# Scores of the first heads set in a fixed order between the last gate products, and the gate and branch instructions around them recorded in program order

## The chip, the cores and the metric

One core of a Trainium2 chip runs the whole program. The metric is the time of one execution in microseconds (us); smaller is better. The engines are PE (matrix multiply), ACT (scalar engine), DVE (vector engine), POOL (GpSimd) and SP, which here only issues DMAs; each works through its own list of instructions in order.

## The reference

One layer of a hybrid encoder, sequence 1024, width 1024, float32:

```python
h = rms_norm(x, norm1)
proj = h @ w_in                       # q, k, v of 16 heads, forget logits, 2 x 1024 gate columns
o_a = forgetting_attention(...)       # 8 causal heads of 64, with cumulated log-forget terms ("fox")
o_b = chunk_band_attention(...)       # 8 heads of 64, own chunk and 8 chunks before, relative bias
g_a, g_b = split(sigmoid(gates), 2)
merged = g_a * (o_a @ w_branch_a) + g_b * (o_b @ w_branch_b)
x = x + merged @ w_out
x = x + square(relu(rms_norm(x, norm2) @ w_up)) @ w_down
return rms_norm(x, final_norm)
```

## The kernel before

**Precision.** Every float32 operand is held as two float32r halves, high and low: `split` writes the high half with an ACT cast and the low half with a subtraction on DVE or POOL. `split_w` does the same to a weight block of 128x512: `wh_...` is cast on ACT, `wl_...` is subtracted on POOL. A product is then three matmuls for each block of 128 rows (high x high, high x low, low x high); 4 blocks make the 12 matmuls that the text counts.

**Stages in order.** Projections to q, k, v; eight gate units; attention of 16 heads (8 of the chunk kind, then 8 of the fox kind); the branch products; the output products (`o`); the feed-forward part. The projections and gates are Strassen products of 7 products of 12 matmuls each for a 2x2 block (operands B11, T1 to T4, B21, B22; weights A11, S1 to S4, A12, A22), accumulated in four PSUM banks `u{unit}_{n}`. A generator, `strassen_steps`, yields after each of the seven. The finished quarter of a gate goes through `gate_out` (`zt`): times `rstd`, a sigmoid on ACT, a store to `z_dram`.

**The gate tail.** Units 6 and 7 are taken last. Unit 7 does its first two products (A11 x B11, S2 x T2), then unit 6 runs `EARLY` = 6 steps. Then T2 and B11 are freed, and in their place `qk` tiles of the first two heads are loaded on POOL's queue. `shifts` computes for a head the scores (`s`, 12 matmuls), reduces each to a minimum on DVE (`mn`), transposes it on PE (`mt`), splits it (`mr`) and stores it to `m_rows`. Attention subtracts it from its own scores (`st`, on PE, with operands `qk` and `sk`) before the exponential (`p`, on ACT), and multiplies by the values (`pv`).

**The branch products.** `branch(pool, b, c, h)` makes `m{c}_{h}_{b}`: weights `wr` are loaded by SP, split to `wh_ab{c}_{b}` and `wl_ab{c}_{b}`, multiplied with the attention output `oh`, `ol` (24 matmuls for both h), and the result is multiplied by the gate `z` on DVE. The branch b = 0 goes between the fox heads as `fillers`; b = 1 comes after attention: there POOL adds (`m`), ACT casts (`mh`), POOL subtracts (`ml`), and `mh`, `ml` are the operands of the output products. Attention's last pair of heads is normalised by `on` (DVE, with `rb` loaded from `r_dram`), stored to `o_dram` by ACT's queue, loaded as `olt` and split to `oh`, `ol`.

**What sets the order.** A scheduler places the instructions of each engine when the program is built; dependences and the order of writing guide it. An engine wrapped by `Ordered` (VO, TO, AO, LO) keeps its instructions among each other in the order in which the program writes them:

```python
return lambda *a, **kw: tc.keep_in_program_order(getattr(self.eng, name)(*a, **kw))
```

Each such instruction has the line of this helper in the profile (L96 before, L95 after). Tiles live in rings: `wr` has 4 buffers (RAW), `wh` and `wl` 6 each (HL).

Of the kernel before, what the change touches and what calls it, by code (L numbers as in the profile page):

```python
# [18 lines left out]
P = 128  # L19
# [12 lines left out]
EARLY_GATES = 2  # L32
START1 = (0,)
START2 = (0, 1, 2, 3)
EARLY, AHEAD = 6, 2
LO_POOL = lambda n: False

BC, PB = 2, 5
# [2 lines left out]

NORM = (2, 6, 10, 14)
BIAS = 1
GPOOL = (7,)

LEAD, XB, XR = 3, 4, 6

# [30 lines left out]
def hs(h):  # L78
    return slice(h * HALF, (h + 1) * HALF)
# [3 lines left out]
def hybrid_block(ctx: ExitStack, tc: tile.TileContext, xT, g1, wall, wf, fb, relb, relt, rows, g2, g3, outT):  # L83
# [20 lines left out]
    def psum(stack, name, bufs):  # L104
        return stack.enter_context(tc.tile_pool(name=name, bufs=bufs, space=PSUM, reuse_waits="tile"))
# [106 lines left out]
    def product(bank, first, pairs, part=False, eng=T):  # L212

        n = len(pairs) * 3
        t = 0
        for w, x in pairs:
            for wi, xi in ((0, 0), (0, 1), (1, 0)):
                eng.matmul(bank, w[wi], x[xi], start=(first and t == 0), stop=(t == n - 1 and not part),  # L218
                         skip_group_check=part or not first)
                t += 1  # L220
# [91 lines left out]
    for h in range(2):  # L312
# [36 lines left out]
    def gate_out(ps, c, h, eng=V):  # L349
        t = etile("zt")  # L350
        eng.tensor_tensor(t, ps, rstd[:, hs(h)], op=ALU.mult)
        A.activation(t, t, AF.Sigmoid)
        store(z_dram[c, :, hs(h)], t)

    def norm1():
# [79 lines left out]
        load_r(qk, qk_dram[2 * pr + hh])  # L435
        return qk

    def shifts(pr, hh, qk, bc, ps_s, ps_t):

        fox = pr >= 4  # L440
        mn = aps.tile([P, 8], F32, tag="mn", name=f"mn{pr}_{hh}", bufs=2)
        for i in range(8):
            j0 = 0 if fox else max(0, i - 4)
            W = (i + 1 - j0) * P
            st = aps.tile([P, 4], F32, tag="st", name="st", bufs=4)
            prev, x = 3.0e38, 0
            for s0, n, v in pieces(W):
                ks = j0 * P + s0
                ps = ps_s.tile([P, HALF], F32, tag="d", name="s")
                diag = fox and s0 + v == W  # L450
                T.matmul(ps[:, :n], qk[:, 1, i * P:(i + 1) * P], qk[:, 0, ks:ks + n], start=True, stop=not diag)  # L451
# [6 lines left out]
                V.tensor_tensor_reduce(ps[:, :v], ps[:, :v], bc[:, b0:b0 + v], 1.0, prev, ALU.add, ALU.min, out)  # L458
# [4 lines left out]
        T.transpose(pt[0:8, 0:P], mn, ident)  # L463
# [7 lines left out]
        for _ in strassen_steps(*args, **kw):  # L471
            pass

    def strassen_steps(u, ps_pool, mk, out, start=(), between=None, before=None, cut=0):
# [9 lines left out]
        for b in (0, 2, 3, 1) if between else range(4):  # L484
            banks[b] = ps_pool.tile([P, HALF], F32, tag="d", name=f"u{u}_{b}")
        p1, u2, c22 = mk("p1"), mk("u2"), mk("c22")
        steps = [(n, range(4)) for n in range(7)]
        if start:
            more = (0, 4, 1, 2, 3, 5, 6) if between else range(7)
            steps = [(n, range(3)) for n in start] + [(n, (3,) if n in start else range(4)) for n in more]  # L490
        for i, (n, ks) in enumerate(steps):
            if i >= cut:
                yield
            if cut and i == cut:
                ws = strassen_w(u, G, ALL[cut:])
            wn, xn, b, first = PRODS[n]
            wh, wl = ws[wn]
            product(banks[b], first and 0 in ks, [((wh[:, k, :], wl[:, k, :]), xop[xn, k]) for k in ks],
                    3 not in ks)
            if 3 not in ks:  # L500
                continue
            if n == 3 and before:
                before[0]()
            if n == 0:
                A.copy(p1, banks[0])
            elif n == 1:
                V.tensor_tensor(u2, banks[1], p1, op=ALU.add)
            elif n == 2:
                V.tensor_tensor(c22, banks[2], u2, op=ALU.add)
            elif n == 3:  # L510
                V.tensor_tensor(c22, banks[3], c22, op=ALU.add)
                out(1, 1, c22)
            elif n == 4:
                if between:
                    between()
                out(0, 0, banks[0])
            else:
                t = mk("cc")
                V.tensor_tensor(t, banks[b], u2, op=ALU.add)  # L519
                out(*((0, 1) if n == 5 else (1, 0)), t)  # L520
        if before:
            before[1]()
            for a in late:
                out_(*a)
# [37 lines left out]

        return finish

    def project_gate(g, **kw):
        return strassen_steps(U_GATE + g, psd[1 - next(units) % 2], etile,
                              lambda row, h, src: gate_out(src, 2 * g + row, h,
                                                          G if g in GPOOL and (row, h) != (0, 0) else V), **kw)

    project_qk(0)  # L570
    for i in range(4):
# [22 lines left out]
    apq = [pool(astack, f"apq{n}", "right") for n in range(2)]  # L594
    for n in range(2):
# [15 lines left out]
    ap_, apv, apq2, ap0 = [pool(astack, n, "right") for n in ("ap", "apv", "apq2", "ap0")]  # L611
    apq.append(apq2)
    psg = psum(astack, "psg", 1)
    pss = psum(astack, "pss", 3)
# [5 lines left out]
    def branch(ps_pool, b, c, h):  # L620

        if h == 0:
            ab_w[b, c] = [split_w(quarter(U_AB + c // 2, ((0, 1), (3, 2))[c % 2][b]), f"ab{c}_{b}")]
        (wh, wl), = ab_w[b, c]
        g = (1 - b) * 8 + c
        z = tmp("z")
        load(z, z_dram[g, :, hs(h)])
        ps = dense(ps_pool, f"m{c}_{h}_{b}", [(wh[:, k, :], wl[:, k, :]) for k in range(4)],
                   [(oh[:, k, hs(h)], ol[:, k, hs(h)]) for k in range(4)])
        V.tensor_tensor(z, ps, z, op=ALU.mult)  # L630
        return z
# [4 lines left out]
        c, h = fillers.pop(0)  # L636
        store(m_dram[c, :, hs(h)], branch(psg, 0, c, h))


    v3 = [apv.tile([P, 8, 3, HD], F32R, tag=f"v3{hh}", name=f"v3{hh}") for hh in range(2)]  # L640
    for hh in range(2):
        V.memset(v3[hh][:, :, 2, :].bitcast(F32), 1.0)

    sks = [ap_.tile([SK, 2, S], F32R, tag=f"sk{n}", name=f"sk{n}") for n in range(2)]

    def load_rest(pr, hh):
        sk = sks[hh]
        if pr % 4 == 0:
            load_r(sk[HD:SK - 2], rows[pr // 4, 0:16])
            load_r(sk[SK - 2:SK, 0, :], rows[pr // 4, 16:18, 0, :])  # L650
        load_r(sk[0:HD], sk_dram[2 * pr + hh])
        load_r(v3[hh][:, :, 0:2, :].rearrange("p c a d -> p c (a d)"), v_dram[pr, hh])
        load_r(sk[SK - 2:SK, 1, :], m_rows[2 * pr + hh])
        return sk

    lo_n, acc_o = [0], {}

    def attend(pr, hh, sk, qk, nb):
# [4 lines left out]
        for h in range(2):  # L663
# [5 lines left out]
            for n, (j, b0, b1) in enumerate(chunks):  # L669
# [28 lines left out]
                A.activation(p[:, c], ps[:, c], AF.Exp, scale=-1.0, bias=ncq[:, j, head:head + 1] if fox else 0.0)  # L698
# [37 lines left out]
                split((oh[:, pr, hs(h)], ol[:, pr, hs(h)]), o, G)  # L736

    forget_columns()
    rest, steps = load_rest(*heads[0]), iter(())
    for n, hd in enumerate(heads):  # L740
        sk, more = rest, iter(())
        if n < 15:
            rest = load_rest(*heads[n + 1])
        if n < 14:
            tiles.append((load_head(*heads[n + 2]), *load_bias(*heads[n + 2])))
            more = shifts(*heads[n + 2], *tiles[-1][:2], pss, psg)
# [370 lines left out]
```

## Time and profile before

| | |
|---|---|
| median of 3 runs | 1561.5 us (1555.68 to 1564.74) |
| the profiled execution | 1553.71 us, its span 1551.9 us (1.8 us lie around it) |
| granted clock of PE, mean | 0.976 |
| busy in the span | PE 1469.4 us (95%), DVE 1018.2 (66%), POOL 919.3 (59%), ACT 735.3 (47%) |

Times within the span are counted from its start. A matmul's row gives the time from issue to its modelled end (0.39 us with 512 columns), while the next is issued earlier: its start minus the start of the row before is what a matmul costs in a row. A row of an engine shows in brackets the idle time before it and what ended it. A row that ends in "xN" stands for N instructions.

### The profile page before, as it was taken

The numbers are of one execution on the slowest core, as the hardware profiler recorded it, in microseconds if no ns is written. First come the engines' busy times: TensorE is split into PE (matmuls) and PEld (weight loads), VectorE is DVE, ScalarE is ACT, GpSimd is POOL, SyncE is SP. The second block draws the span as 40 slices with busy tenths as digits, with TensorE's granted clock in tenths as the row PEclk, the third lists the DMA queues.
The fourth block names the chain that finished last, engine by engine and source line by source line (L and its number), as shares of the span: only waits on it lengthen the run. The fifth ranks groups of instructions, "written<-read, shape, count | busy, mean of one in ns | idle before, by whom it ended". The sixth has DMA issues, their size and how long they took to land.

```text
span 1551.9 us, 21027 instructions
## 1 busy us (share of the span) xinstructions
PE 1469.4 (95%) x6788; PEld 1212.7 (78%) x6788; DVE 1018.2 (66%) x1543; ACT 735.3 (47%) x1379; POOL 919.3 (59%) x735
## 2 busy tenths in 40 slices
PE   6798999999979998999999999999999899999996
PEld 4586888888858787888787888888888688888885
DVE  8989555753356787875422687666666546999644
ACT  5543333334327786766623554333333344444653
POOL 6886776869871222211048378888877445467553
PEclk9799999999989999999999999999999999999998
DMA  4155667774395777885466624444443757489353
GB/s 151 55 150 124 187 186 198 213 214 141 119 270 146 150 166 159 214 214 151 140 196 197 203 68 156 154 152 149 156 151 136 268 187 227 140 251 225 101 188 124
DMA packets 150320, 262.92 MB, mean 169 GB/s; under 512 B 21880, under 2 KB 39544, under 8 KB 147072
## 3 DMA queue, kind: packets, MB, share of 16 engines
q1 hardware_dynamic: 75968, 136.79, 29.0%
q10 hardware_dynamic: 50304, 84.24, 17.0%
q0 software_dynamic: 23936, 40.54, 11.8%
q8 instruction: 53, 0.87, 0.2%
q14 instruction: 59, 0.48, 0.1%
HBM read 175.19 MB, written 86.31 MB: 169 GB/s over the span
## 4 chain that ended last, share of the span: by engine, by line
PE 40%; POOL 3%; DMA 3%; DVE 2%; issue 2%; ACT 1%; SPq 0%; ACTq 0%; DVEq 0%; POOLq 0%
PE u L218 19%; PE dS L218 11%; PE dA L218 5%; PE o L218 4%; POOL wl_A L167 1%; POOL m L785 1%; POOL ml L269 1%; DMA xT<-a_dram 1%; DMA z<-z_dram 1%; PE dA L96 0%; DMA wr<-wall 0%; DMA rb<-r_dram 0%; DVE B22l L269 0%; DVE T2l L269 0%; DMA r_dram<-d 0%
## 5 line engine op out<-in xcount | busy, mean ns | idle before, releaser
L167 POOL TENSOR_TENSOR wl_A<-wr,wh_A 128x512 fp32r<-128x512 f32 x121 | 172.4, 1432 | 61.7 <-ACT wh_A L165 44.2
L167 POOL TENSOR_TENSOR wl_S<-S,wh_S 128x512 fp32r<-128x512 f32 x105 | 146.6, 1399 | 38.3 <-ACT wh_S L165 38.0
L269 DVE TENSOR_TENSOR tl<-p,th 128x512 fp32r<-128x512 f32 (+1 forms) x192 | 110.6, 597 | 29.4 <-ACT th L268 24.5
L165 ACT CAST wh_A<-wr 128x512 fp32r<-128x512 f32 x105 | 65.1, 620 | 103.0 <-DMA a_dram<-at 52.5
L165 ACT CAST wh_S<-S 128x512 fp32r<-128x512 f32 x105 | 64.0, 619 | 78.4 <-PE u L218 33.1
L167 POOL TENSOR_TENSOR wl_S<-ks,wh_S 128x512 fp32r<-128x512 f32 x48 | 68.7, 1512 | 53.8 <-ACT wh_S L96 53.8
L268 ACT CAST th<-p 128x512 fp32r<-128x512 f32 (+1 forms) x192 | 92.3, 508 | 12.2 <-PE pv L702 6.3
L458 DVE CUSTOM_DVE_ANT_0 s<-s,bc 128x384 f32<-128x384 f32 (+3 forms) x128 | 69.6, 562 | 35.2 <-PE s L451 18.5
L451 PE MATMUL s<-qk 128*128 128x384 f32 (+2 forms) x192 | 64.5, 368 | 23.7 <-DMA qk<-qk_dram 13.7
L519 DVE TENSOR_TENSOR cc<-u,u 128x512 f32<-128x512 f32 x70 | 47.9, 686 | 54.9 <-PE u L218 54.6
L188 POOL TENSOR_TENSOR S<-wr,wr 128x512 f32<-128x512 f32 x36 | 51.7, 1436 | 45.4 <-DMA wr<-wall 38.1
L167 POOL TENSOR_TENSOR wl_A<-ka,wh_A 128x512 fp32r<-128x512 f32 x32 | 45.2, 1422 | 47.1 <-ACT wh_A L96 47.1
L880 ACT ACTIVATE v<-v 128x512 f32<-128x512 f32 x64 | 40.5, 632 | 67.4 <-DVE v L879 64.6
L686 PE MATMUL st<-sk 82*128 82x512 f32 (+1 forms) x192 | 66.5, 347 | 1.1 <-DMA sk<-m_rows 1.1
L678 PE MATMUL st<-qk 128*128 128x512 f32 (+1 forms) x192 | 66.9, 352 | 0.2 <-ACT p L698 0.2
L701 PE MATMUL pv<-th,v 128*128 128x512 f32 (+1 forms) x192 | 65.6, 342 | 1.1 <-ACT on L714 0.6
L703 PE MATMUL pv<-tl,v 128*128 128x512 f32 (+1 forms) x192 | 65.4, 340 | 0.9 <-DVE tl L269 0.8
L702 PE MATMUL pv<-th,v 128*64 128x512 f32 (+1 forms) x192 | 65.0, 339 | 0.0
L268 ACT CAST qkh<-qk 128x512 fp32r<-128x512 f32 x32 | 19.9, 621 | 95.1 <-DMA qk_dram<-qkl 41.2
L698 ACT ACTIVATE p<-st,ncq 128x512 f32<-128x512 f32 (+1 forms) x96 | 54.1, 598 | 21.2 <-PE st L694 15.4
L451 PEld LDWEIGHTS s<-qk 128*128 128x128 f32 x192 | 36.8, 201 | 33.1 <-issue 7.9
L208 POOL TENSOR_TENSOR S<-wr,S 128x512 f32<-128x512 f32 x35 | 49.6, 1418 | 17.8 <-DMA wr<-wall 14.3
(378 smaller groups left out, 5082.5 us busy)
## 6 DMA issues: line engine op xcount, KB each, us to landing
wr<-wall SPq DMA_DIRECT2D x243, 256.0 KB
qk<-qk_dram POOLq DMA_DIRECT2D x16, 1024.0 KB, 6.1
a_dram<-at ACTq DMA_DIRECT2D x64, 256.0 KB
xT<-a_dram SPq DMA_DIRECT2D x64, 256.0 KB
qk_dram<-qkh ACTq DMA_DIRECT2D x96, 128.0 KB
a_dram<-v ACTq DMA_DIRECT2D x48, 256.0 KB
xB<-a_dram SPq DMA_DIRECT2D x44, 256.0 KB
z_dram<-zt ACTq DMA_DIRECT2D x32, 256.0 KB
```

Of the source, the lines that this page charges most:

```text
L165: act.copy(wh, src)
L167: G.tensor_tensor(wl, src, wh.bitcast(F32), op=ALU.subtract)
L218: eng.matmul(bank, w[wi], x[xi], start=(first and t == 0), stop=(t == n - 1 and not part), skip_group_check=part or not first)
L268: A.copy(dst[0], src)
L269: eng.tensor_tensor(dst[1], src, dst[0].bitcast(F32), op=ALU.subtract)
L451: T.matmul(ps[:, :n], qk[:, 1, i * P:(i + 1) * P], qk[:, 0, ks:ks + n], start=True, stop=not diag)
L458: V.tensor_tensor_reduce(ps[:, :v], ps[:, :v], bc[:, b0:b0 + v], 1.0, prev, ALU.add, ALU.min, out)
L678: T.matmul(ps[:, c], qk[:, 0, keys], qk[:, 1, qs], start=True, stop=False)
L686: T.matmul(ps[:, c], sk[:, 0, keys], sk[:, 1, qs], start=False, stop=not extra)
L701: T.matmul(pv[:, c], v3[hh][:, j, 1:3, :], th[:, c], start=first, stop=False)
L702: T.matmul(pv[0:HD, c], v3[hh][:, j, 0, :], th[:, c], start=False, stop=False)
L703: T.matmul(pv[:, c], v3[hh][:, j, 1:3, :], tl[:, c], start=False, stop=last)
```

## The change

1. `EARLY` goes from 6 to 3; unit 7, unit 6 and the `shifts` of the first two heads issue their matmuls through `TO`, so that PE keeps the order written. Two scores and then four stand between products.
2. PSUM is shared out anew for the gate tail: one bank `psl`, four `psu`, three `psa` for scores. `strassen_steps` takes its banks one by one.
3. The first head's `sk` and `v3` tiles move to the pool `ap1`, in the place of T2 and B11, and are loaded on POOL's queue before the last gate weights; the load of its row of minima is a call of its own (`load_shift`).
4. GPOOL is dropped: all `zt` products go to DVE.
5. The sigmoids of unit 7 and the first exponentials are issued through `AO`. So is the cast in `split_w` for all branch weights.

```diff
-EARLY, AHEAD = 6, 2
+EARLY, AHEAD = 3, 2
...
-GPOOL = (7,)
...
-    last = project_gate(7, cut=2)
+    pstack.close()
+    lstack = ExitStack()
+    psl, psu, psa = [psum(lstack, n, b) for n, b in (("psl", 1), ("psu", 4), ("psa", 3))]
+    last = project_gate(7, [psl, psa, psu, psu], cut=2, eng=TO)
     next(last)
-    steps = project_gate(6)
+    steps = project_gate(6, [psu] * 4, eng=TO)
     for _ in range(EARLY):
         next(steps)
     xtop.close()
     apq = [pool(astack, f"apq{n}", "right") for n in range(2)]
+    ap1 = pool(astack, "ap1", "right")
...
+    head_tiles(ap1)
     for n in range(2):
         tiles[n] = (load_head(*heads[n]), *tiles[n])
-    ahead = chain(*[shifts(*heads[n], *tiles[n][:2], psd[1], psd[1]) for n in range(2)])
+    rest = load_rest(*heads[0])
+    ahead = chain(*[shifts(*heads[n], *tiles[n][:2], psa, psa, TO) for n in range(2)])
     for _ in chain(steps, last):
         for _ in range(AHEAD):
             next(ahead, None)
     for _ in ahead:
         pass
-    pstack.close()
+    load_shift(*heads[0])
+    lstack.close()
...
-            ab_w[b, c] = [split_w(quarter(U_AB + c // 2, ((0, 1), (3, 2))[c % 2][b]), f"ab{c}_{b}")]
+            ab_w[b, c] = [split_w(quarter(U_AB + c // 2, ((0, 1), (3, 2))[c % 2][b]), f"ab{c}_{b}", AO)]
...
-                A.activation(p[:, c], ps[:, c], AF.Exp, scale=-1.0, bias=ncq[:, j, head:head + 1] if fox else 0.0)
+
+                exp = (A if pr or hh or h or n else AO).activation
+                exp(p[:, c], ps[:, c], AF.Exp, scale=-1.0, bias=ncq[:, j, head:head + 1] if fox else 0.0)
```

**PE in the gate tail.** Before, around the first score of the first head (`s` on `qk0_0`), which stands behind the sixth product (B22 with S4) of unit 6:

```order
L218 MATMUL u6_2_3856<-B22h_130,wl_6_S4_3848 128x512
L451 MATMUL s_3967<-qk0_0_3943 128x256
L218 MATMUL u6_3_3857<-T4h_122,wh_6_A22_3850 128x512
L218 MATMUL u6_3_3857<-T4l_126,wh_6_A22_3850 128x512
L218 MATMUL u6_3_3857<-T4h_122,wl_6_A22_3852 128x512
```

And at the end of the tail, where all scores of the second head (`qk0_1`) follow the last gate product:

```order
L218 MATMUL u7_3_3782<-T4h_122,wl_7_A22_4024 128x512
L463 MATMUL mt_4108<-ident_66,mn0_0_3965 8x128
L451 MATMUL s_4134<-qk0_1_3945 128x256
L451 MATMUL s_4138<-qk0_1_3945 128x256
L451 MATMUL s_4160<-qk0_1_3945 128x384
L451 MATMUL s_4164<-qk0_1_3945 128x512
```

Now the first score stands behind the third product (T1 with S1) of unit 6, three products earlier:

```order
L95 MATMUL u6_2_3918<-T1h_154,wl_6_S1_3843 128x512
L95 MATMUL s_3934<-qk0_0_3910 128x256
L95 MATMUL s_3938<-qk0_0_3910 128x256
L95 MATMUL u6_3_3941<-T3h_146,wh_6_S3_3846 128x512
L95 MATMUL u6_3_3941<-T3l_150,wh_6_S3_3846 128x512
```

and the last of the second head ahead of unit 7's last product:

```order
L95 MATMUL s_4195<-qk0_1_3912 128x256
L95 MATMUL mt_4198<-ident_66,mn0_1_4101 8x128
L95 MATMUL u7_3_4110<-T4h_122,wh_7_A22_4083 128x512
L95 MATMUL u7_3_4110<-T4l_126,wh_7_A22_4083 128x512
```

So scores that stood in a block behind the gates stand between the gate products, while the load of `qk` keeps its place on POOL (behind `wl_6_S4`).

**ACT after attention.** `wh_ab{c}_1` are the casts of b = 1 weights, `mh` the casts of the sums. Before, the last two of the eight weight casts stand ahead of the first `mh`, and then only `mh` follow:

```order
L268 CAST oh_4217<-olt_8352 128x512
L165 CAST wh_ab6_1_8648<-wr23_1_8646 128x512
L165 CAST wh_ab7_1_8696<-wr23_2_8694 128x512
L268 CAST mh0_8322<-m_8356 128x512
```

Now `wh_ab7_0`, the last of b = 0, stands behind the store of the normalised heads, `wh_ab0_1` behind all casts of `olt`, and each later one behind both `mh` of the c before:

```order
L755 DMA o_dram_102<-on7_1_8049 128x512
L95 CAST wh_ab7_0_8271<-wr23_3_8269 128x512
...
L267 CAST oh_4240<-olt_8364 128x512
L95 CAST wh_ab0_1_8372<-wr20_1_8370 128x512
L671 DMA m_dram_106<-z_8292 128x512
L267 CAST mh0_8334<-m_8368 128x512
L267 CAST mh1_8329<-m_8395 128x512
L95 CAST wh_ab1_1_8420<-wr20_2_8418 128x512
L267 CAST mh0_8334<-m_8416 128x512
L267 CAST mh1_8329<-m_8443 128x512
L95 CAST wh_ab2_1_8468<-wr21_1_8466 128x512
```

What moved: seven weight casts, from ahead of the sums to one between each two pairs of sums.

**POOL and PE after attention.** On POOL the same order, before:

```order
L167 TENSOR_TENSOR wl_ab4_1_8554<-wr22_1_8550,wh_ab4_1_8552 128x512
L167 TENSOR_TENSOR wl_ab5_1_8602<-wr22_2_8598,wh_ab5_1_8600 128x512
L785 TENSOR_TENSOR m_8356<-m_8356,z_8364 128x512
L167 TENSOR_TENSOR wl_ab6_1_8650<-wr23_1_8646,wh_ab6_1_8648 128x512
```

and now:

```order
L166 TENSOR_TENSOR wl_ab0_1_8374<-wr20_1_8370,wh_ab0_1_8372 128x512
L807 TENSOR_TENSOR m_8368<-m_8368,z_8376 128x512
L268 TENSOR_TENSOR ml0_8335<-m_8368,mh0_8334 128x512
L807 TENSOR_TENSOR m_8395<-m_8395,z_8397 128x512
L268 TENSOR_TENSOR ml1_8330<-m_8395,mh1_8329 128x512
L166 TENSOR_TENSOR wl_ab1_1_8422<-wr20_2_8418,wh_ab1_1_8420 128x512
```

PE before takes the products of four c at once (here the second half, h = 1):

```order
L218 MATMUL m0_1_1_8387<-oh_4217,wh_ab0_1_8360 128x512
L218 MATMUL m1_1_1_8435<-oh_4217,wh_ab1_1_8408 128x512
L218 MATMUL m2_1_1_8483<-oh_4217,wh_ab2_1_8456 128x512
L218 MATMUL m3_1_1_8531<-oh_4217,wh_ab3_1_8504 128x512
```

and now one c after the other; two matmuls of each h need only `wh`, the other ten of each stand behind the first that needs `wl`:

```order
L217 MATMUL m1_0_1_8426<-oh_4240,wh_ab1_1_8420 128x512
L217 MATMUL m1_0_1_8426<-ol_4241,wh_ab1_1_8420 128x512
L217 MATMUL m1_1_1_8447<-oh_4240,wh_ab1_1_8420 128x512
L217 MATMUL m1_1_1_8447<-ol_4241,wh_ab1_1_8420 128x512
L217 MATMUL m1_0_1_8426<-oh_4240,wl_ab1_1_8422 128x512
```

What moved: four c in parallel became one c at a time, each behind its own `wl`.

More of the change, by code (lines that the diff above doesn't have):

```diff
@@ L348, in hybrid_block, with gate_out @@
         store(c_dram[:, hs(h)], z)
[L349 removed]
+    def gate_out(ps, c, h, act=A):
         t = etile("zt")
[L351 to L352 removed]
+        V.tensor_tensor(t, ps, rstd[:, hs(h)], op=ALU.mult)
+        act.activation(t, t, AF.Sigmoid)
         store(z_dram[c, :, hs(h)], t)
@@ L436, in load_head, with shifts @@
         return qk
-    def shifts(pr, hh, qk, bc, ps_s, ps_t):
+    def shifts(pr, hh, qk, bc, ps_s, ps_t, T=T):
         fox = pr >= 4
@@ L472, in strassen_unit, with strassen_steps @@
             pass
-    def strassen_steps(u, ps_pool, mk, out, start=(), between=None, before=None, cut=0):
+    def strassen_steps(u, ps_pool, mk, out, start=(), between=None, before=None, cut=0, eng=T):
         ws = strassen_w(u, G, ALL[:cut] if cut else FIRST if between else ALL)
@@ L483, in strassen_steps, with bank @@
         banks = {}
-        for b in (0, 2, 3, 1) if between else range(4):
-            banks[b] = ps_pool.tile([P, HALF], F32, tag="d", name=f"u{u}_{b}")
+        def bank(b):
+            if b not in banks:
+                banks[b] = (ps_pool[b] if isinstance(ps_pool, list) else ps_pool).tile(
+                    [P, HALF], F32, tag="d", name=f"u{u}_{b}")
+            return banks[b]
+        for b in (0, 2, 3, 1) if between else () if isinstance(ps_pool, list) else range(4):
+            bank(b)
         p1, u2, c22 = mk("p1"), mk("u2"), mk("c22")
@@ L497, in strassen_steps @@
             wh, wl = ws[wn]
-            product(banks[b], first and 0 in ks, [((wh[:, k, :], wl[:, k, :]), xop[xn, k]) for k in ks],
-                    3 not in ks)
+            product(bank(b), first and 0 in ks, [((wh[:, k, :], wl[:, k, :]), xop[xn, k]) for k in ks],
+                    3 not in ks, eng)
             if 3 not in ks:
@@ L563, in project_v, with project_gate @@
         return finish
[L565 to L568, printed above, removed]
+    def project_gate(g, banks=None, **kw):
+        return strassen_steps(U_GATE + g, banks or psd[1 - next(units) % 2], etile,
+                              lambda row, h, src: gate_out(src, 2 * g + row, h, AO if g == 7 else A), **kw)
     project_qk(0)
@@ L594, in hybrid_block, with head_tiles, load_rest, load_shift @@
     apq = [pool(astack, f"apq{n}", "right") for n in range(2)]
+    ap1 = pool(astack, "ap1", "right")
+    sks, v3 = [], []
+    def head_tiles(p):
+        n = len(sks)
+        sks.append(p.tile([SK, 2, S], F32R, tag=f"sk{n}", name=f"sk{n}"))
+        v3.append(p.tile([P, 8, 3, HD], F32R, tag=f"v3{n}", name=f"v3{n}"))
+        V.memset(v3[n][:, :, 2, :].bitcast(F32), 1.0)
+    def load_rest(pr, hh):
+        sk = sks[hh]
+        if pr % 4 == 0:
+            load_r(sk[HD:SK - 2], rows[pr // 4, 0:16])
+            load_r(sk[SK - 2:SK, 0, :], rows[pr // 4, 16:18, 0, :])
+        load_r(sk[0:HD], sk_dram[2 * pr + hh])
+        load_r(v3[hh][:, :, 0:2, :].rearrange("p c a d -> p c (a d)"), v_dram[pr, hh])
+        return sk
+    def load_shift(pr, hh):
+        load_r(sks[hh][SK - 2:SK, 1, :], m_rows[2 * pr + hh])
+    head_tiles(ap1)
     for n in range(2):
         tiles[n] = (load_head(*heads[n]), *tiles[n])
-    ahead = chain(*[shifts(*heads[n], *tiles[n][:2], psd[1], psd[1]) for n in range(2)])
+    rest = load_rest(*heads[0])
+    ahead = chain(*[shifts(*heads[n], *tiles[n][:2], psa, psa, TO) for n in range(2)])
     for _ in chain(steps, last):
@@ L610, in hybrid_block @@
     ol = opool.tile([P, 4, S], F32R, tag="ol", name="ol")
-    ap_, apv, apq2, ap0 = [pool(astack, n, "right") for n in ("ap", "apv", "apq2", "ap0")]
+    ap_, apq2, ap0 = [pool(astack, n, "right") for n in ("ap", "apq2", "ap0")]
     apq.append(apq2)
@@ L637, in filler @@
         store(m_dram[c, :, hs(h)], branch(psg, 0, c, h))
[L640 to L654, printed above, removed]
+    head_tiles(ap_)
     lo_n, acc_o = [0], {}
@@ L738, in hybrid_block @@
     forget_columns()
-    rest, steps = load_rest(*heads[0]), iter(())
+    steps = iter(())
     for n, hd in enumerate(heads):
@@ L743, in hybrid_block @@
             rest = load_rest(*heads[n + 1])
+            load_shift(*heads[n + 1])
         if n < 14:
```

## The prediction

> **What bounds the kernel now.** I read the page's first parts, then the busy time by stretches, then the two places where the order of the change differs: the waits of PE in the gate tail, and groups, timelines and the chain of waits after attention.
>
> Stretches, with busy time of each engine, number of instructions, granted clock of PE, DMA share and rate:
>
> ```profile
> span 1551.9 us, 21027 instructions
> PE 1469.4 (95%) x6788; PEld 1212.7 (78%) x6788; DVE 1018.2 (66%) x1543; ACT 735.3 (47%) x1379; POOL 919.3 (59%) x735
> 415.00:450.00 35.00, 34.85 (x158) 28.70 (x156) 21.24 (x39) 11.09 (x20) 29.15 (x30) 1.00 0.71 187
> 450.00:470.00 20.00, 7.45 (x27) 5.06 (x28) 7.58 (x30) 3.44 (x7) 7.72 (x7) 0.64 0.98 254
> 470.00:770.00 300.00, 283.15 (x1586) 244.20 (x1585) 213.30 (x583) 218.54 (x478) 64.26 (x93) 0.97 0.68 168
> 770.00:845.00 75.00, 70.14 (x305) 55.97 (x303) 20.30 (x29) 21.24 (x35) 49.23 (x40) 1.00 0.65 205
> 845.00:900.00 55.00, 55.00 (x244) 45.57 (x243) 36.32 (x50) 30.96 (x54) 24.58 (x17) 1.00 0.55 180
> ```
>
> PE bounds nearly everything; the one hole of weight is 450 to 470 (PE 7.45 of 20 us, clock 0.64), the end of the gates. From 770 to 900, the branch and output products, PE is nearly full at full clock. A change can gain at most the hole, and can lose much where PE is full. Its two halves fall on just these places.
>
> PE's waits from 415 to 475, and the ACT and PE rows behind the largest:
>
> ```profile
> PE s L451 <- DMA qk<-qk_dram: 5.1, 1, 5.1
> PE s L451 <- DVE mr L269: 4.7, 1, 4.7
> PE mt L463 <- DVE mn L458: 2.4, 2, 1.3
> 456.45 0.62 ACT L165 CAST wh_ab<-wr 128x512 fp32r<-128x512 f32 x1 [8.56 <-DMA wr<-wall]
> 456.98 0.25 ACT L268 CAST mr<-mt 8x128 fp32r<-8x128 f32 x1
> 423.24 0.39 PE L218 MATMUL u<-T3h,wh_S 128*128 128x512 f32 x1
> 424.57 1.31 POOL L435 DMA_DIRECT2D qk<-qk_dram  x2
> DMA to landing us min/median/max: 5.9/8.8/16.0
> 449.46 0.39 PE L218 MATMUL u<-T4h,wl_A 128*128 128x512 f32 x1
> 469.29 1.33 PE L678 MATMUL st<-qk 128*128 128x512 f32 x3
> 469.37 1.28 ACT L698 ACT_TABLE_LOAD   x1 [0.67 <-DVE mr L269]
> ```
>
> The gates end at 449.85 and attention starts at 469.29. Between them the second head's scores wait for `mr`, whose ACT cast stands behind a branch weight's cast that waits 8.56 us for its load, and for a third head's `qk` (load in 16.0 us).
>
> **Part A, the gate tail.** Removed: these waits. The branch casts of b = 0 leave the tail, the second head's scores go among the products. Three `zt` products move from POOL (off the path) to DVE, about 0.7 us each on an engine 21.24 of 35 us busy: no cost on the path, at worst 2 us if a score's reduction is behind them. The first head's `sk` and `v3` loads put four more DMA issues on POOL ahead of `wl_7_S1`, under the wait of PE that follows.
>
> Added: that wait. The first score now stands where T3 stood, at 423.24. Its `qk` is issued at 424.57, in the same place of POOL's list as before, and lands 5.9 us later: 430.5. PE idles 7.3 us. Then come 449.85 - 423.24 = 26.6 us of products and first-head scores as before, 1.8 us for the second head's 12 scores (3,968 columns at 0.2275 us for 512), some 1.0 us for the transposes. After the wait the clock is half for a while, as here after 455:
>
> ```profile
> 452.60:456.00 3.40, 0.32 (x2) 0.07 (x1) 0.00 (x0) 0.00 (x0) 3.30 (x3) 0.94 1.09 286
> 459.40:462.80 3.40, 0.00 (x0) 0.00 (x0) 0.76 (x4) 0.63 (x1) 0.00 (x0) 0.50 1.15 412
> 469.60:473.00 3.40, 3.40 (x16) 3.21 (x15) 0.23 (x2) 2.52 (x4) 0.51 (x1) 0.56 0.41 152
> 473.00:476.50 3.50, 3.50 (x23) 3.12 (x22) 2.50 (x10) 3.47 (x10) 0.29 (x2) 1.00 0.04 9
> ```
>
> PE works at half clock for 3 to 4 us after it is busy again; that loses 2 to 3 us, say 2.4. Last, the scores wait on three banks, each held until its reduction is done:
>
> ```profile
> L458 DVE CUSTOM_DVE_ANT_0 s<-s,bc 128x384 f32<-128x384 f32 (+3 forms) x128 | 69.6, 562 | 35.2 <-PE s L451 18.5
> ```
>
> Of four scores in a row the fourth waits for the first reduction (twice a head, about 1.2 us), and the transpose for the last four (4 x 0.562 = 2.25): about 4.6 us a head, 9.2 in all, an estimate from that row. Sum: 430.6 + 26.6 + 1.8 + 1.0 + 2.4 + 9.2 = 471.6 against 469.29, so +2. From below: if reductions hide under the half-clocked products, 9.2 goes, -7; from above: DVE's other work between the reductions doubles part of it (+4.6), and the first exponential, now ordered behind unit 7's last sigmoid, starts its table load up to 1.4 us later: +8. I take +2, as the reductions are in one chain on one engine.
>
> **Part B, the branch products.** This is the larger half and rests on one word, the `AO` in `split_w`. It keeps each branch weight's cast in program order with the other ordered ACT instructions, and the scheduler now leaves `wh_ab7_0` behind the stores of `on`, `wh_ab0_1` behind all casts of `olt`, and each later cast behind both `mh` of the c before. What these rest on before:
>
> ```profile
> 775.34 1.07 PE L218 MATMUL m<-oh,wh_ab 128*128 128x512 f32 x4
> 786.09 1.31 DVE on L732 x2
> 787.48 2.04 DMA o_dram<-on
> 789.59 2.69 DMA olt<-o_dram
> 791.67 1.32 ACT L268 CAST oh<-olt 128x512 fp32r<-128x512 f32 x2 [11.03 <-DMA olt<-o_dram]
> L218 PE MATMUL m<-oh,wl_ab 128*128 128x512 f32 x70 | 27.1, 389 | 0.0
> L269 POOL TENSOR_TENSOR ml<-m,mh 128x512 fp32r<-128x512 f32 x16 | 20.7, 1313 | 0.0
> L785 POOL TENSOR_TENSOR m<-m,z 128x512 f32<-128x512 f32 x16 | 20.7, 1306 | 19.7 <-DVE z L630 19.7
> L630 DVE TENSOR_TENSOR z<-m,z 128x512 f32<-128x512 f32 x18 | 12.5, 692 | 38.6 <-DMA z<-z_dram 35.5 <-PE m L218 3.1
> L268 ACT CAST mh<-m 128x512 fp32r<-128x512 f32 x16 | 9.9, 621 | 29.6 <-POOL m L785 29.6
> L167 POOL TENSOR_TENSOR wl_ab<-wr,wh_ab 128x512 fp32r<-128x512 f32 x3 | 3.9, 1299 | 9.0 <-ACT wh_ab L165 9.0
> 842.33 57.92 PE o L218 x254
> ```
>
> Before, PE begins the b = 1 products at 775.34, under the 16 us in which the last pair is normalised and fetched, since their weights have long been split (three of the eight `wl_ab` are left in this stretch). POOL's additions follow behind, and PE takes output products meanwhile. The chain of waits leaves PE at 842.33 and runs through 254 of its output matmuls to 900.25. That is 57.92 / 254 = 0.228 us a matmul.
>
> Now, step by step. (1) `wh_ab7_0` can be cast only when `on` is done, 787.4 and a store's issue: 788.6 at its end, its `wl` at 790. PE stands idle from about 770 (the end of attention and m6) to then. (2) The load of a later branch weight (`wr21_2`) is in SP's list ahead of the last two `olt` loads and waits for the buffer of `wr23_3`, which `wl_ab7_0` frees: so `olt` is issued at 790.1 and not 789.0, lands 2.7 to 3.3 us later, 793.4. (3) On ACT a store of z (m7_0, 12 matmuls at half clock from 789, 5.1 us, 0.7 on DVE: 795.2) and four casts of `olt` at 0.62 stand ahead of `wh_ab0_1`: 798.3 at its end, `wl_ab0_1` starts at 798.4.
>
> (4) Then a ring of dependences for each c: `wl_ab` 1.30; ten matmuls that need it, 9 x 0.2275 + 0.39 = 2.44; z 0.69; POOL `m` 1.30; ACT `mh` 0.62; POOL `ml` 1.25 (its pitch back to back, just under the 1.31 of the row); `m` of h = 1 1.30; `mh` 0.62; `ml` 1.25; and the hand-overs, some 0.4. Together 11.2 us at full clock. The next `wh` cast goes beside the last `ml`, so it is free. PE has 24 matmuls in each, 5.5 us. It idles 4 to 5 us in every round.
>
> (5) Those pauses are as long as a slice of the table above in which PE did nearly nothing, after which the clock was half. At half clock the ten matmuls cost 2.0 us more, and if the second ten are slow as well, z of h = 1 comes later than POOL is free, 0.9 more: 13.2 to 14.1 us a round. After a stretch of steady work the clock returns (473.00), so some matmuls are fast in each round. I take 12.5, nearer to the slow case because the row at 469.60 shows the first work after a pause at half clock.
>
> The Trainium skill (TensorE: Matmul & The Clock Gate, "HAM oscillation — how this bites in real kernels") speaks against this change: no pause of PE over about 3.4 us, else each following piece of work starts cold, every time. By that rule every round has its ten slow matmuls: 13.2 us, and the sum would be 1639 in place of 1634. The trace's rows agree on one pause (0.50 in 459.40); no row before shows a pause that recurs.
>
> (6) Seven rounds: `wl_ab7_1` starts at 798.4 + 87.5 = 885.9, ends 887.2. Behind it PE has 20 branch and 376 output matmuls, 396 x 0.2275 = 90.1 us, plus 1.5 for a slow start: 978.8, against 900.25: +78.6. Nothing of it can run before: all output products need sums over every c but eight matmuls that stand earlier. POOL's last `m` and `ml` come within 13 us of `wl_ab7_1` and PE has other c's output matmuls for that time, so they add nothing. Behind 900 the program is the same, and shifts.
>
> (7) In the fox heads the b = 0 casts and `wl_ab` come just ahead of their products. POOL has room there, 64.26 of 300 us busy in attention, and this is how it waits for a cast already:
>
> ```profile
> 765.74 1.30 POOL L167 TENSOR_TENSOR wl_ab<-wr,wh_ab 128x512 fp32r<-128x512 f32 x1 [17.78 <-ACT wh_ab L165]
> ```
>
> So I put it at 0, from -2 to +4, bounded by one pair of `wh` and `wl` (1.9 us) being late at two of the eight fillers.
>
> Sum: 1553.71 + 2 + 78.6 = 1634.3. The profiled execution is 7.8 us under the median of 1561.5; the runs span 9 us, so I keep the profiled basis and let the range carry that.
>
> **Rivals.**
>
> - R1, no slow clock: rounds of 11.2 us. `wl_ab7_1` ends at 878.1, PE at 968.2: +68, total 1624. For it: PE's pause is split by four `wh` matmuls, so a stretch of 3.4 us need not be empty. Against: the slices 452.60 and 469.60.
> - R2, the slow clock in every round, 13.2 to 14.1: PE ends at 984 to 990, total 1639 to 1645.
> - R3, rounds bound by POOL alone, five operations of 1.25 = 6.25 us: it would need the second half's sum and the next `wl_ab` not to wait on ACT or PE. PE ends at 798.4 + 43.8 + 1.3 + 90.1 = 933.6: +33, total 1589. POOL was back to back before, but with four c in flight; now the order has one.
> - R4, the other side: faster. Place: the gate tail, 450 to 470. If `qk` is there in time (no 7.3 us wait, no 2.4 of slow clock) attention starts at 462 and A is -7.5 or, with reductions hidden too, -16.7. It decides only where B costs less than that, which needs rounds under about 4 us (798.4 + 7 x 4 + 91.4 = 917.8, +17.5), shorter than POOL's own 6.25; so also the ACT order above would have to not bind. Total 1537 to 1550.
> - R5, the change does not reach the branch: the time is A's alone, 1547 to 1562, about the same.
>
> **Chances.** Forecast (12 to 13.2 us a round) 0.50; R1 0.14; R2 0.18; R3 0.08; R4 0.05; R5 0.05. Within 0.5% counts as same, about what a measurement of this kernel can tell. Slower 0.90, same 0.05, faster 0.05. The range takes the forecast, R1 with A's lower end (1624 - 9 = 1615, rounded to 1612) and R2 with some of A's upper end (1645 + 7): 1612 to 1652.
>
> **What would show it.** PE idle from about 770 to 788, released by ACT `wh_ab`; then eight bursts of 24 branch matmuls, 11 to 14 us apart, with clock under 1 there; POOL `wl_ab` in the stretch eight times, each ending an idle time that ACT's cast ends; PE's last output matmul near 979. In the tail: a wait of PE for `qk` near 423, of about 7 us, and attention's first `st` between 462 and 477. The prediction is wrong if casts of later c run ahead of the `mh`, or if PE has output products to do in the pauses.

## The result, and the profile after

The changed kernel takes 1627.47 us (median of 4 runs, 1623.31 to 1630.32), the kernel before beside it 1558.59 (4 runs). The ratio is 1.0439, with a 95% interval of 1.0388 to 1.0489: slower. The forecast was 1634 (1612 to 1652). The profiled execution is one of these runs, 1630.32 us, the highest; that of the kernel before, 1553.71, is near the lowest of its own. So the two profiles lie 76.6 us apart and the medians 68.9; what follows on the profiles accounts for the former.

The first lines of the page of the changed kernel, and its busy time by stretches (columns as before: PE, PEld, DVE, ACT, POOL, clock, DMA share, rate):

```profile
span 1628.3 us, 21030 instructions
PE 1495.7 (92%) x6788; PEld 1224.0 (75%) x6788; DVE 1014.8 (62%) x1546; ACT 736.9 (45%) x1379; POOL 915.7 (56%) x732
450.00:470.00 20.00, 16.75 (x71) 13.35 (x71) 11.58 (x34) 2.78 (x5) 3.58 (x6) 0.92 0.79 190
470.00:770.00 300.00, 277.30 (x1542) 236.75 (x1541) 209.72 (x578) 214.14 (x467) 62.96 (x92) 0.96 0.70 164
770.00:800.00 30.00, 15.07 (x63) 11.01 (x62) 7.36 (x13) 8.68 (x18) 2.57 (x2) 0.80 0.45 139
800.00:890.00 90.00, 60.72 (x187) 42.86 (x185) 15.90 (x24) 16.01 (x27) 40.87 (x33) 0.80 0.40 126
```

The hole at 450 to 470 is filled (PE 16.75 of 20 us, before 7.45), with gate products that now run later. A larger one has opened from 770 to 890, where PE does only 187 matmuls in the 90 us from 800 on, at clock 0.80. Who is waited for there, from 765 to 895 (us in all, times, longest):

```profile
PE m L217 <- ACT wh_ab L95: 44.8, 9, 13.6
PE m L217 <- DVE z L664: 0.8, 1, 0.8
PE m L217 <- POOL wl_ab L166: 0.7, 1, 0.7
```

Nine waits for the ordered casts: one of 13.6 us for `wh_ab7_0`, one of 1.2 for `wh_ab0_1`, and seven of about 4.3, one in each of the seven rounds that follow. POOL's timeline shows one of these rounds, from one `wl_ab` to the next:

```profile
818.95 1.28 POOL L166 TENSOR_TENSOR wl_ab<-wr,wh_ab 128x512 fp32r<-128x512 f32 x1
824.37 1.29 POOL L807 TENSOR_TENSOR m<-m,z 128x512 f32<-128x512 f32 x1 [4.14 <-DVE z L664]
826.39 1.26 POOL L268 TENSOR_TENSOR ml<-m,mh 128x512 fp32r<-128x512 f32 x1 [0.73 <-ACT mh L267]
827.61 1.26 POOL L807 TENSOR_TENSOR m<-m,z 128x512 f32<-128x512 f32 x1
829.60 1.27 POOL L268 TENSOR_TENSOR ml<-m,mh 128x512 fp32r<-128x512 f32 x1 [0.73 <-ACT mh L267]
830.83 1.28 POOL L166 TENSOR_TENSOR wl_ab<-wr,wh_ab 128x512 fp32r<-128x512 f32 x1
```

The ring begins and ends at these rows of POOL, the first idle behind the long wait of ACT, and the chain of waits leaves through PE's output matmuls:

```profile
796.16 0.62 ACT L95 CAST wh_ab<-wr 128x512 fp32r<-128x512 f32 x1 [14.38 <-DVE on L753]
807.26 1.81 POOL L166 TENSOR_TENSOR wl_ab<-wr,wh_ab 128x512 fp32r<-128x512 f32 x1 [9.13 <-ACT wh_ab L95]
894.35 1.28 POOL L166 TENSOR_TENSOR wl_ab<-wr,wh_ab 128x512 fp32r<-128x512 f32 x1
902.72 74.36 PE o L217 x328
```

Seven rounds in 894.35 - 807.26 = 87.09 us, 12.44 each. The same point that PE passed at 842.33 + 57.92 = 900.25 before is now 902.72 + 74.36 = 977.08: 76.8 us later, and the whole span is 76.4 longer. All of the loss is there by then; nothing is lost or won behind it.

The gate tail after, PE's waits from 415 to 480 and the first matmuls of scores and of attention:

```profile
PE s L95 <- DMA qk<-qk_dram: 7.5, 1, 7.5
PE s L95 <- DVE st L457: 3.4, 4, 0.9
PE mt L95 <- DVE mn L457: 3.1, 2, 1.6
431.35 0.77 PE L95 MATMUL s<-qk 128*128 128x256 f32 x2 [7.49 <-DMA qk<-qk_dram]
472.15 0.50 PE L697 MATMUL st<-qk 128*128 128x512 f32 x1
```

The waits for `mr` and for a third head's `qk` are gone; one for the first head's `qk`, three products earlier, has taken their place. Attention begins 2.9 us later than before (469.29).

### The profile page after: what moved, and what is told of

Its sections match the earlier page's. It is cut to its first block, busy times and chain, and to the rows that moved or that the text cites. A ratio compares the mean times of both kernels' runs of the same rounds, so it can differ in the third digit from the quotient of the medians.

```text
span 1628.3 us, 21030 instructions
## 1 busy us (share of the span) xinstructions
PE 1495.7 (92%) x6788; PEld 1224.0 (75%) x6788; DVE 1014.8 (62%) x1546; ACT 736.9 (45%) x1379; POOL 915.7 (56%) x732
## 4 chain that ended last, share of the span: by engine, by line
PE 71%; DVE 8%; issue 8%; DMA 6%; POOL 3%; ACT 2%; ACTq 0%; SPq 0%; DVEq 0%; POOLq 0%
PE u L217 35%; PE dS L217 11%; PE dA L217 7%; PE o L217 5%; DMA qk<-qk_dram 3%; PE m L217 3%; PE u L95 2%; PE s L450 1%; PE dA L95 1%; POOL m L807 1%; PE pv L722 1%; PE pv L724 1%; PE pv L723 1%; DMA m_rows<-mr 1%; PE st L697 1%
## 5 line engine op out<-in xcount | busy, mean ns | idle before, releaser
L217 PE MATMUL m<-oh,wh_ab 128*128 128x512 f32 x128 | 60.0, 469 | 45.6 <-ACT wh_ab L95 44.8
L664 DVE TENSOR_TENSOR z<-m,z 128x512 f32<-128x512 f32 x32 | 22.1, 691 | 100.6 <-PE m L217 88.7
L217 PEld LDWEIGHTS m<-oh,wh_ab 128*128 128x128 f32 x128 | 28.8, 225 | 55.1 <-ACT wh_ab L95 48.6
L450 PE MATMUL s<-qk 128*128 128x512 f32 (+2 forms) x168 | 55.6, 358 | 14.5 <-DMA qk<-qk_dram 9.3
```

## The experiments

Theory: the loss is the ring that the ordered casts (`AO` in `split_w`) make behind attention, and it needs nothing else of the change; the new gate tail by itself is worth little. Rivals: the tail, its PSUM split or the moved tiles; and, within the ring, whether the clock matters. Ratios are to the kernel before in the same group, with 95% intervals; a "+n us" is that ratio's share of the 1554 to 1555 us which the kernel before takes in these groups.

### One word taken away, one word added

**e1**: the changed kernel with the branch casts free.

```diff
-            ab_w[b, c] = [split_w(quarter(...), f"ab{c}_{b}", AO)]
+            ab_w[b, c] = [split_w(quarter(...), f"ab{c}_{b}")]
```

> The changed kernel with one word undone: the branch weights' casts go through A again, so the scheduler may place them early; the gate tail keeps the new order. Theory (the ordered casts make a ring of waits behind attention, and only that costs): the stage after attention is as before, output products reach their end 0 to 3 us later than 900, and the time is that of the kernel before plus what the gate tail alone is worth: attention begins at about 472 as in the changed kernel, so +3 us, -3 to +6. Rival (the new gate tail, its PSUM split or the moved tiles lengthen attention by themselves): +8 us or more, with fox heads slower. Rival (the ring comes from something else in the change): still +60 or more.

Measured 1558.93 us, ratio 1.0034 (1.0018 to 1.0051), +5 us, inside the expected -3 to +6. There is no ring; the last two `wl_ab` follow close upon each other:

```profile
800.42 1.29 POOL L166 TENSOR_TENSOR wl_ab<-wr,wh_ab 128x512 fp32r<-128x512 f32 x1
802.92 1.30 POOL L166 TENSOR_TENSOR wl_ab<-wr,wh_ab 128x512 fp32r<-128x512 f32 x1
```

Attention begins at 470.66, its last `pv` is at 773.80 (before 770.28), and PE passes the point that it passed at 900.25 before at 904.02, 3.8 us later (expected 0 to 3).

**e2**: the kernel before with that word added, and nothing else.

```diff
-            ab_w[b, c] = [split_w(quarter(...), f"ab{c}_{b}")]
+            ab_w[b, c] = [split_w(quarter(...), f"ab{c}_{b}", AO)]
```

> The kernel before with one word added: the branch weights' casts through AO, nothing else. Theory: the ring appears whole, seven rounds of 11.2 to 13.2 us between the POOL subtractions of b = 1, mean near the 12.4 of the changed kernel, and the time is 70 to 80 us over the kernel before; the gate tail is 3 to 5 us shorter than before, because no branch cast stands ahead of mr. Rival (the ring needs the new tail's order too): within 10 us of the kernel before.

Measured 1616.98 us, ratio 1.0417 (1.0376 to 1.0457), +65 us. The first and last rows of POOL's ring, and the stretch between them:

```profile
790.86 1.81 POOL L167 TENSOR_TENSOR wl_ab<-wr,wh_ab 128x512 fp32r<-128x512 f32 x1 [9.37 <-ACT wh_ab L96]
878.16 1.28 POOL L167 TENSOR_TENSOR wl_ab<-wr,wh_ab 128x512 fp32r<-128x512 f32 x1
790.86:878.16 87.30, 56.24 (x170) 40.05 (x171) 10.36 (x16) 13.07 (x23) 44.42 (x36) 0.80 0.37 117
```

Seven rounds in 87.30 us, against 87.09 in the changed kernel. The two experiments together show it: the word makes the ring, with the tail or without. The expected 70 to 80 us were a little too many: attention ends earlier here (last `pv` at 763.73), and the ring starts 16.4 us earlier than in the changed kernel. The gate tail missed its expectation: attention begins at 467.40, 1.9 us earlier than before and not 3 to 5. The wait for `mr` is gone, but PE waits 9.1 us for `qk`.

### Half of the word

**e3**: `A if b else AO` in place of `AO`, so only the casts of b = 0 are ordered. **e4**: `AO if b else A`, so only those of b = 1.

> The changed kernel with AO for the weights of b = 0 only, and A for b = 1. In its order wh_ab7_0 stays behind the stores of the normalised heads, but the casts of b = 1 follow at once and PE takes four c at a time. Theory (two separate prices: about 18 us of PE's idle time before wh_ab7_0, and the ring): no ring, branch products without gaps after about 790, +18 to +30 us over the kernel before. Rival (the idle time before wh_ab7_0 is hidden in the normalising of the last pair, only the ring costs): +3 to +8.

> The changed kernel with AO for the weights of b = 1 only, and A for b = 0. In its order the casts of b = 0 are early again, and wh_ab0_1 stands behind all olt casts, each later one behind both mh of the c before. Theory: the ring stays, seven rounds of 11.5 to 13.2; it starts some 7 to 10 us earlier than in the changed kernel (at 797 to 800), since the last olt loads and casts no longer wait for wh_ab7_0: +60 to +70 us over the kernel before. Rival (the ring's cost is mostly the late start): +30 or less.

e3: 1582.71 us, ratio 1.0187 (1.0156 to 1.0218), +29. e4: 1620.03 us, ratio 1.0437 (1.0402 to 1.0472), +68. POOL in e3 (one row for five subtractions) and the ring's start in e4:

```profile
797.26 6.66 POOL L166 TENSOR_TENSOR wl_ab<-wr,wh_ab 128x512 fp32r<-128x512 f32 x5 [20.68 <-ACT wh_ab L95]
791.02 1.27 POOL L166 TENSOR_TENSOR wl_ab<-wr,wh_ab 128x512 fp32r<-128x512 f32 x1 [53.35 <-ACT wh_ab L95]
```

In e3 no ring follows, but it is some 24 us slower than e1. Two things differ in the traces: everything of b = 1 waits behind `wh_ab7_0` until 797 (PE's wait is 13.1 us), and attention itself ends 7.2 us later (last `pv` at 780.95). In e4 the ring starts at 791.02, 16 us earlier than in the changed kernel, and takes 88.46 us to its last `wl_ab` at 879.48. In the timed runs the two prices do not add up: e4 and the changed kernel have the same ratio (1.0437 and 1.0439, each to about half a per cent). The profiled execution of e4, 1615.04 us, is the lowest of its four runs (up to 1625.03) and that of the changed kernel the highest, so some of the 16 us may be spread between executions; how much of it the timed runs have is not settled.

### The clock within the ring

**e5**: 20 more matmuls behind the branch products of each c below 7, into a bank that nothing reads.

```diff
+            if h == 1 and c < 7:
+                (wh, wl), = ab_w[1, c]
+                dm = psm[0].tile([P, HALF], F32, tag="d", name=f"dm{c}")
+                for _ in range(20):
+                    T.matmul(dm, wl[:, 3, :], oh[:, 3, hs(1)], start=True, stop=True)
```

> The changed kernel, with 20 matmuls more of 512 columns behind the branch products of each c below 7 (into a bank that nothing reads), so that PE has no long pause in a round; they are extra work, 140 matmuls. Theory (a round is 11.2 us of hand-overs and the rest, about 1.2 us, is PE at half clock after its pause): clock 1.0 from the second round on, rounds of 11.0 to 11.4, the time 6 to 9 us below the changed kernel. Rival (rounds are 12.4 by contention or hand-overs, clock or not): rounds stay, time the same. Rival (the extra matmuls stand in the way of the next c): rounds longer.

The ring of the changed kernel, its fastest and slowest middle rounds, and the ring of e5:

```profile
807.26:894.35 87.09, 56.20 (x170) 39.92 (x171) 10.36 (x16) 13.08 (x23) 44.49 (x36) 0.80 0.37 118
843.58:856.75 13.17, 8.87 (x26) 6.30 (x25) 1.38 (x2) 1.76 (x3) 6.29 (x7) 0.76 0.31 99
856.75:868.54 11.79, 7.48 (x26) 5.32 (x25) 1.38 (x2) 1.75 (x3) 6.26 (x6) 0.79 0.37 113
810.36:889.78 79.42, 73.44 (x311) 57.41 (x312) 10.36 (x16) 13.16 (x23) 44.93 (x35) 1.00 0.42 129
```

With 140 matmuls more, the seven rounds take 7.7 us less: 11.35 each, at clock 1.00 (11.77 the first, 11.24 to 11.29 the others). DVE, ACT and POOL do the same work in both. So a PE that idles about 4.3 us in each round pays about 1.1 us a round for its slow clock. The expected 6 to 9 us of the whole time do not show: 1624.16 us, ratio 1.0458 (1.0428 to 1.0489), against 1.0439 (1.0388 to 1.0489) for the changed kernel, which can't be told apart. In this profile the ring began 3.1 us later (attention at 474.53), which took part of the gain.

### The gate tail

**e6** is e1 once more, a single run, as the base of this group (whatever its label says, nothing else is changed). **e7** is e1 with `EARLY` 5 in place of 3. **e8** is e1 with the first two heads' `qk` through SP's queue:

```diff
-    def load_head(pr, hh):
+    def load_head(pr, hh, q=None):
...
-        load_r(qk, qk_dram[2 * pr + hh])
+        if q is None:
+            load_r(qk, qk_dram[2 * pr + hh])
+        else:
+            q.dma_start(qk.bitcast(F32), qk_dram[2 * pr + hh])
...
-        tiles[n] = (load_head(*heads[n]), *tiles[n])
+        tiles[n] = (load_head(*heads[n], nc.sync), *tiles[n])
```

**e11** is e1 with unit 7's sigmoids and the first exponentials through A, not AO.

> The kernel of e1 again, one look, as the base of this group: attention begins at 470 to 472, PE waits 5 to 8 us for the first qk, total 3 to 6 us over before.

> e1 (branch casts free) with EARLY 5 in place of 3: the first scores stand two products later on PE (5.4 us), the last four scores and the transpose of the second head after the last gate product. Theory (the gain of the new order is eaten by the wait for qk and the slow clock after it): the wait falls from 5.4-7.5 us to under 2, no half clock in 426 to 436, but the tail's last reductions (about 3 us) stand open before attention; attention begins at 465 to 469, total 0 to 4 us below the kernel before. Rival (the reductions of the scores are what holds the tail): attention begins at 470 to 473, total as e1.

> e1 (branch casts free) with the first two heads' qk loaded through SP's queue instead of POOL's; the order on PE stays that of the changed kernel. Theory (qk is issued at 424.6 only because three POOL subtractions stand ahead of it, while its place is free at 420.8): issued near 421, the wait of PE falls to 2-4 us and the half clock after it goes or halves, attention begins at 464 to 468, total 0 to 4 us below the kernel before. Rival (the load is bound by the DMA queues' other traffic, or SP waits for a weight buffer ahead of it): wait as in e1, total as e1.

> e1 (branch casts free) with the sigmoids of unit 7 and the first exponentials through A as well, so that of the ACT part nothing is ordered. Theory (of the tail's +5 us, 1.5 to 2 come from the first exponential behind the last sigmoid and its store): the wait of st for p falls from 2.1 to under 1, total 1 to 2 us below e1. Rival (nothing in it): as e1.

| | ratio, 95% interval | wait for the first `qk` | attention begins |
|---|---|---|---|
| e1 | 1.0034 (1.0018 to 1.0051) | 5.4 us | 470.66 |
| e6 | one run, 1558.96 us | 7.6 | 470.04 |
| e7 | 1.0027 (1.0009 to 1.0044) | 2.8 | 471.00 |
| e8 | 1.0035 (1.0018 to 1.0052) | 5.1 | 470.72 |
| e11 | 1.0057 (1.0033 to 1.0080) | 8.2 | 472.57 |

e1 and e6 are one program, so a difference of 2 us in the wait is within the spread. My theory of e7 falls: the wait for `qk` went from 5.4 and 7.6 to 2.8 us, the clock was 1.00 from 426 to 436, as expected, and attention began no earlier. What took its place in e7 (PE's rows):

```profile
431.05 0.47 PE L95 MATMUL s<-qk 128*128 128x256 f32 x2 [2.82 <-DMA qk<-qk_dram]
445.39 0.58 PE L95 MATMUL s<-qk 128*128 128x256 f32 x1 [4.81 <-DVE st L457]
470.20 0.27 PE L95 MATMUL mt<-ident,mn 128*8 128x128 f32 x1 [1.07 <-DVE mn L457]
```

A wait for a reduction on DVE, and the last transpose right ahead of attention.

e8 does not test what it was meant to. SP (waits from 415 to 423) has two weight loads ahead of `qk`, which wait for a free buffer, so `qk` is issued at 422.31; in e1 POOL issues it at 422.54. The rival, that SP waits for a weight buffer ahead of it, came true, and what an earlier issue would bring is not shown.

```profile
SPq L159 <- POOL wl_S L166: 5.3, 1, 5.3
SPq L159 <- POOL wl_A L166: 5.2, 1, 5.2
422.31 0.90 SPq L437 DMA_DIRECT2D qk<-qk_dram  x2
```

e11's theory falls too: the wait of `st` for `p` was 1.1 us, against 2.1 in e1 and 1.5 in e6 (expected under 1), but the kernel is not faster.

### The casts written earlier

In **e9** (on the changed kernel) and **e10** (on the kernel before) the casts stay ordered, but branch c writes the split of c + 3; **e12** is e10 with five ahead.

```diff
         if h == 0:
-            ab_w[b, c] = [split_w(quarter(...), f"ab{c}_{b}", AO)]
+            for n in range(8 * b + c, min(8 * b + c + 3, 15) + 1):
+                b_, c_ = divmod(n, 8)
+                if (b_, c_) not in ab_w:
+                    q = quarter(U_AB + c_ // 2, ((0, 1), (3, 2))[c_ % 2][b_])
+                    ab_w[b_, c_] = [split_w(q, f"ab{c_}_{b_}", AO)]
```

> The changed kernel with its ordered branch casts, but each written three branches earlier in the program (the split of c + 3 is written where branch c begins). Theory (an ordered cast keeps the place where it is written, and that place made the ring): no ring of single rounds, c's in pairs, POOL near back to back after about 797; wh_ab7_0 stands before attention's end, so no idle of 14 us before it; 3 to 12 us over the kernel before. Rival (order as such costs, wherever written): +40 or more.

> The kernel before with the branch casts ordered and written three branches earlier; its gate tail keeps its own order of scores. Theory: the branch casts are out of the gate tail, so mr no longer waits behind them; attention begins at 466 to 468, and behind attention c's run in pairs: between -5 and +6 us of the kernel before. Rival (POOL's loads for the heads stand behind wl_ab as in the changed kernel): attention ends 5 or more us later, +8 or more.

> As e10 with five branches ahead: four c's in flight on PE behind attention as in the kernel before, and all casts of b = 0 in the fox heads. Theory: branch and output products as before, POOL's loads for the heads less held up than in e10, attention begins at 466 to 468: 1 to 6 us below the kernel before. Rival (a cast waiting for its buffer holds the exponentials behind it on ACT): PE waits for p in the fox heads, +3 or more.

e9: 1571.04 us, ratio 1.0100 (1.0078 to 1.0123), some 16 us, more than the 3 to 12 expected; its attention ends late, the last `pv` at 783.18, for a reason that is not settled. e10: 1.0027 (1.0009 to 1.0045), inside its range. e12: 1.0016 (0.9997 to 1.0034), which can't be told from no change and is not the 1 to 6 us below that were expected. The ring is gone in all three though every cast is ordered: the last `wl_ab` starts at 832.22, 821.74 and 814.13, in the changed kernel at 894.35. It is the place where a cast is written that made the ring. None beats the kernel before, and attention does not begin at 466 to 468, as expected, in e10 (475.54, with a wait of 10.7 us for `qk`) or in e12 (470.72). In e12 the branch casts are out of the gate tail and `mr` no longer waits, but PE's waits from 415 to 480 show where that time went:

```profile
PE s L451 <- DMA qk<-qk_dram: 10.7, 2, 10.5
PE mt L463 <- DVE mn L458: 2.4, 2, 1.3
470.72 0.80 PE L682 MATMUL st<-qk 128*128 128x512 f32 x1
```

One wait of 10.5 us for the third head's `qk` in place of 4.7 for `mr` and 5.1 for `qk`: the same load ends the tail, cast or not.

## Why the prediction was right

**Right in sign and place, and in size partly by luck.** The loss lies in part B, by the ring of step (4), and e1 and e2 show that the one word makes it. The parts of the sum, with A's 2 us added to every time behind it:

| step | forecast | measured |
|---|---|---|
| A, attention begins | +2 (471.6) | +2.9 (472.15) |
| wait for the first `qk` | 7.3 us | 7.5 |
| first `wl_ab` of the ring, (3) and A | 800.4 | 807.26 |
| a round, (5) | 12.5 us | 12.44 |
| from the last `wl_ab` to the shared point, (6) | 92.9 us | 82.7 |
| PE at that point, with A | 980.8 | 977.1 |

**Two terms were mis-sized, and they cancel in part.** Step (6) counted all 376 output matmuls that remain, but set the end against 900.25, the point where the chain leaves PE for `B21h`. At that point 48 output matmuls are still to come, in both kernels; the chain after shows 328 and not 376. The last output matmul, before and after:

```profile
910.73 0.39 PE L218 MATMUL o<-mh,wl_o 128*128 128x512 f32 x1
987.56 0.39 PE L217 MATMUL o<-mh,wl_o 128*128 128x512 f32 x1
```

That is 48 x 0.2275 = 10.9 us too many: counted to the same instruction, the sum would have been 1623 and not 1634, against a profiled 1630.32. What hid this is the ring's start, which came 6.9 us later than the sum had it. A is 0.9 of this. The rest is step (7), which I had at 0 (-2 to +4): attention itself, from its first `st` to its last `pv`, took 307.9 us (472.15 to 780.08) against 301.0 (469.29 to 770.28), with fewer branch matmuls in it. From there to the ring it took 27.2 us, 0.9 less than forecast.

The ordered casts of b = 0 are what lengthens attention in the new frame: e4 differs from the changed kernel in its b = 0 casts alone, and its attention takes 300.7 us (470.23 to 770.95); in e3 and e5, which order them, it takes 309.9 and 309.1. One way in which they do it is seen in the changed kernel: POOL waits for a cast on ACT, and the loads for a head stand behind it.

```profile
731.21 1.29 POOL L166 TENSOR_TENSOR wl_ab<-wr,wh_ab 128x512 fp32r<-128x512 f32 x1 [16.31 <-ACT wh_ab L95]
732.45 0.55 POOL L619 DMA_DIRECT2D sk<-sk_dram  x1
732.99 0.53 POOL L624 DMA_DIRECT2D sk<-m_rows  x1
741.62 0.47 PE L705 MATMUL st<-sk 82*128 82x512 f32 x1 [3.19 <-DMA sk<-m_rows]
```

I bounded (7) by the lateness of the weights themselves and left out what stands behind `wl_ab` on POOL. PE's wait of 3.2 us is part of the 6.9; what makes up the rest is not settled, nor why e2, which orders the same casts in the old frame, has only 296.3 us of attention.

**Step (5), the slow clock.** The hand-overs were read rightly: 11.2 us forecast, 11.24 to 11.29 in e5 at full clock. The 12.5 was a choice between this and the slow case, and it met the mean of 12.44: rounds took 11.69 to 13.17 us, neither R1 (11.2 each) nor R2 (13.2 to 14.1 each). The Trainium skill (TensorE: Matmul & The Clock Gate, "HAM oscillation — how this bites in real kernels") has each piece of work start cold after a pause of PE over about 3.4 us, every time. Here PE's pauses in the ring were about 4.3 us and the granted clock was below 1 in every one of the six full rounds from 818.95 to 894.35 (0.76 to 0.79), and e5, without the pauses, ran at 1.00 with 11.35. So every piece does start slow; but by the prediction's estimate for that rule every round would be 13.2, and rounds of 11.79 and 11.88 show that the slow stretch can end early within the ten matmuls that matter. In the round from 843.58 all ten follow at 0.43 us or more, in the round from 856.75 only the first three, and the others at 0.23.

**Part A.** Its size was right, its working less so: the waits behind reductions were 6.5 us (3.4 and 3.1), not 9.2, and there was a second stretch at a lower clock, 0.68 from 465 to 470, that the sum did not have. e1 prices A over the whole program at +5 us, and e7, e8 and e11 find no part of it whose removal gains. R3, R4 and R5 did not happen.

## What to carry to other kernels

Pinning an instruction to its written place can cost much where the scheduler used to pull it ahead (e2, +65 us by one word), and little where it is written early enough (e10 and e12, within 0.3%): before pinning a helper, find all its callers and where each stood in the old order. When a weight's cast moves behind the result of the round before, a pipeline becomes a ring, and its period is the sum of all hand-overs. At full clock it could be read off the order and the rows of single operations to within 1% (11.2 us against 11.24 to 11.29); the slow clock's share could only be bounded. When comparing two end points, count the work up to the same instruction in both.

## What the runs showed that was not expected

More work made a stage shorter: 140 extra matmuls took 7.7 us out of seven rounds, since PE's clock stayed at 1.00 in place of 0.80. And PE's wait for `qk` in the gate tail was 2.8 us in e7, 5 to 8 in e1, e6, e8 and e11, and 10.5 in e12, with attention beginning between 470.0 and 472.6 in all six (outside these, at 467.40 in e2, 468.54 in e9 and 475.54 in e10); where rows were compared (e7, e12), the wait that was removed had come back on the next operand in line. Profiles of the same instructions differ here by a few us themselves: attention begins at 472.15 in the changed kernel and at 474.53 in e5, whose extra matmuls come behind attention.
